# Four modulation rows moved from the projection stage into the key and value stage of a diffusion block

## The chip, the cores and the metric

One Trainium2 chip, one core. The metric is the device time of one launch in microseconds (us). The kernel is written for a scheduler: it records operations in program order, and a list scheduler sets the order of each engine's queue before the run. On the chip each engine then runs its own queue strictly in that order, and waits at an instruction until its operands are there. The engines are PE (TensorE, matmuls), DVE (VectorE), ACT (ScalarE), POOL (GpSimd) and SP, whose queue here only issues DMAs. ACT also issues DMAs, between its own instructions.

## What is computed

One layer of a hybrid block over 1024 latent tokens with 256 context tokens, model width 1024, all in float32. Cut to what matters here:

```python
sh_a, sc_a, g_a, sh_f, sc_f, g_f = modulation(c, w_mod, b_mod)      # silu(c) @ w_mod + b_mod, six rows of 1024
z = modulate(h, sh_a, sc_a) @ w_in                                  # normed tokens times one wide projection
cq, ckv, kpe, su, gm, gs = split(z)
q, k, v = mla_project(cq, ckv, kpe, ...)                            # keys and values from a compressed kv
att = block_attention(q, k, v)
s5 = s5_mixer(su_lat, su_ctx, ...)                                  # state space branch, both directions
h = layer_norm(ALPHA * h + g_a * branch_merge(att, s5, gm, gs, ...), ln1)
h = layer_norm(ALPHA * h + g_f * peer(modulate(h, sh_f, sc_f)), ln2)
```

Of the six modulation rows the first two (`sh_a`, `sc_a`) are needed before anything else. The last four (`g_a`, `sh_f`, `sc_f`, `g_f`) are first needed after attention. They come from a weight of 16 MB, `w_mod_b`, held as [2, 8, 128, 4, 512]: two halves `r` of two rows each, eight blocks `k` of 128 inputs.

## The kernel before

The tokens are ten tiles of 128: tiles 0 and 1 context, 2 to 9 latent. Four stages matter here.

**Start (to about 54 us).** `w_mod_a` (8 MB) is read and the first two rows are made (`pmr`, line 281).

**Projection stage (to about 182 us).** `project(n)` (lines 301 to 334) normalizes a token tile, transposes it on PE (`tp`, line 191), applies scale and shift into a tile `hm` on ACT (line 317) and DVE (line 319), writes `hm` to DRAM as `hm_d[n]`, and multiplies it by the state space part of `w_in` (`pc`, line 326, 32 matmuls). The result `su` goes to DRAM as `us_d`; for a context tile ACT issues eight small DMAs for that (line 332), for a latent tile one (line 334). Two buffers hold `hm`. After each tile two steps of `modulation_rows` are recorded (`MSTEP = 2`). One step reads 1 MB of `w_mod_b` into one of the four shared weight buffers `w` and runs four matmuls `pr` (line 348), each with a single column of `sil` as its stationary operand, in the four 32-column strips of PE side by side. After eight steps four DVE instructions add the bias (line 354) and the rows go to DRAM as `mod_d`. The first two state space parts (`s5_build`, matmuls `pk` line 519 and `pp` line 538) are also scheduled into this stage.

**Key and value stage (to about 470 us).** Lines 645 to 650 load two weights and then the state space inputs `U`, in eight DMAs of 384 KB, one for each of eight token phases `l`; each takes `us_d` rows of 768 bytes. `U` shares its place in memory with the projection weight `w1`, so it can't be written before the last `pc` has read `w1`. The eighth phase of `U` also needs the last `us_d` write. Then, for each tile `n`, the loop records `s5_states` (`pS`, lines 581 and 582, read `U`), `s5_build` for the next part, `s5_out` (a long row of DVE instructions, then `pY`, lines 620 to 622, then transposes `ptg`, line 637), `compress(n)` (reads `hm_d[n]` back into the `hm` buffers at line 663, matmuls `pb`, line 667, transposes `pt`, line 684), `values` (`pv`, line 695) and `keys` (`pk` from `ckvT`, line 704). DMAs of the tables `T` (line 532) wait on SP for small tables written by ACT.

**Attention of the first token tile** begins with `pa` (line 769), which reads `hm_d[2]` through a weight buffer. Three more groups of tiles, the expert retrieval and its dense part follow; they make up the rest of the time.

Of the kernel before, what the change touches and what calls it, by code (L numbers as in the profile page):

```python
# [8 lines left out]
F32 = mybir.dt.float32  # L9
# [8 lines left out]
MUL, ADD, SUB = ALU.mult, ALU.add, ALU.subtract  # L18
# [3 lines left out]
NT = 10  # L22
# [18 lines left out]
HMB = 2  # L41
# [14 lines left out]
GSTEP = 10  # L56
LSTEP = 24
RSTEP = 4
MSTEP = 2
XLOAD = 4  # L60
GSIDE = ('right', 'right', 'right', None)
CSIDE = ("right", "right", "right", None)
# [26 lines left out]
def block_kernel(ctx: ExitStack, tc: tile.TileContext, a: dict, out: bass.AP):  # L89
    nc = tc.nc  # L90
    V, S, PE, GP, SY = nc.vector, nc.scalar, nc.tensor, nc.gpsimd, nc.sync

    def pool(name, bufs=1, side=None, space=None):
        kw = {"name": name, "bufs": bufs}
        if side:
            kw["side"] = side
        if space is not None:
            kw["space"] = space
        return tc.alloc_tile_pool(**kw)
# [16 lines left out]
    eye = const.tile([128, 128], F32, tag="eye", name="eye")  # L116
# [7 lines left out]
    hm_d = tc.dram_tile([NT, 128, 8 * 128], F32, name="hm_d")  # L124
# [3 lines left out]
    mod_d = tc.dram_tile([4, D], F32, name="mod_d")  # L128
# [74 lines left out]
    def wload(src, shape):  # L203

        t = W.tile([128, 2048], F32, tag="w", bufs=WBUFS, name="w")
        n = 1
        for d in shape[1:]:
            n *= d
        names = "abcd"[:len(shape) - 1]
        dims = {names[i]: shape[i + 1] for i in range(len(names))}  # L210
        flat = " ".join(names)
        v = t[:, 0:n] if len(shape) == 2 else t[:, 0:n].rearrange(f"p ({flat}) -> p {flat}", **dims)
        last[0] = SY.dma_start(v, src)
        return v

    s5 = pool("s5")
# [6 lines left out]
    def bank(tag, name, shape=(128, 512)):  # L223

        if tag == "mm":
            turns[0] ^= turns[1]
            tag = "mm%d" % turns[0]
        return psum.tile(list(shape), F32, tag=tag, bufs={"S": 3, "acc": 2}.get(tag, 1), name=name)
# [104 lines left out]
        else:  # L333
            S.dma_start(us_d[:, :, lat, 32:160].rearrange("b p j -> p b j"), su)


    def modulation_rows():

        rows, brow = (s5.tile([128, 4, 160], F32, tag=t, bufs=2, name="rows").rearrange("p a b -> p (a b)")[:, 0:512]
                      for t in ("gr", "gi"))  # L340
        for r in range(2):
            ps = bank("acc", "pr")
            for j in range(4):
                SY.dma_start(brow[32 * j:32 * j + 1, :], a["b_row"][r, j:j + 1, :])
            for k in range(8):
                wt = wload(a["w_mod_b"][r, k], [128, 4, 512])
                for j in range(4):
                    PE.matmul(ps[32 * j:32 * j + 1, :], sil[:, k, 0:1], wt[:, j, :],
                              start=(k == 0), stop=(k == 7), tile_position=(0, 32 * j))
                yield  # L350
            for j in range(4):
                row = 2 * r + j // 2
                sl = slice(32 * j, 32 * j + 1)
                V.scalar_tensor_tensor(rows[sl, :], ps[sl, :], 1.0 if row == 2 else 0.0, brow[sl, :],
                                       op0=ADD, op1=ADD)
                SY.dma_start(mod_d[row:row + 1, (j % 2) * 512:(j % 2) * 512 + 512], rows[sl, :])

    side = modulation_rows()
    for n in range(NT):
        project(n)  # L360
        for _ in range(MSTEP):
            next(side, None)
    for _ in side:
        pass

    V.tensor_scalar(cni, cni, -1.0, None, op0=MUL)
    kf, kr, ki, pw2 = c32("kf"), c32("kr"), s5.tile([128, 32], I32, tag="ki", name="ki"), c32("pw2")
# [276 lines left out]

    w1b = [wload(a["w_in1"][:, k:k + 4, 0:384], [128, 4, 384]) for k in (0, 4)]
    wk = [wload(a["w_ukv"][:, k, :], [128, 2048]) for k in range(2)]
    U = s5.tile([128, 32, 192], F32, tag="U", name="U")
    ul = us_d.rearrange("b (g c) l j -> l c (b g) j", c=16)
    for l in range(8):
        SY.dma_start(U[16 * l:16 * l + 16], ul[l])  # L650


    SY.dma_start(qng, a["q_norm_g"])
# [5 lines left out]
    def compress(n):  # L659
        lat = n - 2  # L660
        ctxt = lat < 0
        hm = pre.tile([128, 8, 128], F32, tag="hm", bufs=HMB, name="hm")
        SY.dma_start(hm.rearrange("p a b -> p (a b)"), hm_d[n])
        pb = bank("mm", "pb")
        w = 320 if ctxt else 384
        for k in range(8):
            PE.matmul(pb[:, 0:w], hm[:, k, :], w1b[k // 4][:, k % 4, 0:w], start=(k == 0), stop=(k == 7))
        junk = pre.tile([128, 256], F32, tag="junk", name="junk")
        ss = cols.tile([128, 1], F32, tag="ss", name="ss")
        S.activation(junk, pb[:, 0:256], func=AF.Square, accum_out=ss)  # L670
        rk = rstd_of(ss, EPS, 1.0 / 256)
        nrm = pre.tile([128, 384], F32, tag="nrm", bufs=2, name="nrm")
        S.activation(nrm[:, 0:256], pb[:, 0:256], func=AF.Copy, scale=rk)
        if ctxt:
            S.copy(nrm[:, 256:320], pb[:, 256:320])
            S.copy(nrm[:, 320:384], pb[:, 256:320])
        else:
            tmp = pre.tile([128, 128], F32, tag="ktmp", name="ktmp")
            V.tensor_tensor(tmp, pb[:, 256:384], ropt[:, lat, :], op=MUL)
            V.tensor_tensor(nrm[:, 256:320], tmp[:, 0:64], tmp[:, 64:128], op=ADD)  # L680
            S.copy(nrm[:, 320:384], nrm[:, 256:320])
        pt = bank("S", "pt2", (128, 4, 128))
        for j in range(3):
            PE.transpose(pt[:, j, :], nrm[:, j * 128:(j + 1) * 128], eye)
        ko = n * 128
        for j in range(2):
            S.activation(ckvT[:, j, ko:ko + 128], pt[:, j, :], func=AF.Copy, scale=kng[:, j:j + 1])
        S.copy(kpe_h[:, ko:ko + 128], pt[:, 2, :])
        V.tensor_tensor(kpe_l[:, ko:ko + 128], pt[:, 2, :], kpe_h[:, ko:ko + 128].bitcast(F32), op=SUB)
# [11 lines left out]
    def keys(h, c0, c1):  # L701
        ps = bank("mm", "pk")
        for k in range(2):
            PE.matmul(ps[:, 0:c1 - c0], wk[k][:, h * 128:(h + 1) * 128], ckvT[:, k, c0:c1],
                      start=(k == 0), stop=(k == 1))
        kt = pre.tile([128, 512], F32, tag="kv", bufs=3, name="kt")
        S.copy(kt[:, 0:c1 - c0], ps[:, 0:c1 - c0])
        S.dma_start(k_d[h, :, c0:c1], kt[:, 0:c1 - c0])

    for n in range(NT):  # L710
        if n < 8:
            s5_states(n, parts[n])
        if n < 7:
            parts.append(s5_build(n + 1))
        if 0 < n < 9:
            s5_out(n - 1, parts[n - 1])
        compress(n)
        if n:
            values(n - 1)
        for c, n0, n1 in ((0, 4, 8), (1, 8, 10)):  # L720
            if n0 <= n < n1:
                for h in range(8 * (n - n0) // (n1 - n0), 8 * (n - n0 + 1) // (n1 - n0)):
                    keys(h, 512 * c, 512 * c + 512)
    values(NT - 1)
    for h in range(8):
        keys(h, 1024, KEYS)
    s5.release()
    pre.release()

# [857 lines left out]
```

## Time and profile before

| what | value |
|---|---|
| time, median of 3 runs | 3889.87 us (3882.73 to 3898.87) |
| time of the profiled execution | 3890.37 us |
| its span, first to last instruction | 3888.6 us |
| PE busy | 3431.8 us (88% of the span) |
| DVE busy | 3037.1 us (78%) |
| ACT busy | 1645.2 us (42%) |
| POOL busy | 1443.5 us (37%) |
| bytes moved | 1032.55 MB, mean 266 GB/s |
| mean granted TensorE clock | 0.936 of 2.4 GHz |

The shares are means over stages with different limits, so a change inside one stage is read from the rows of that stage. In a timeline row the first number is the start, the second the length, both in us; in square brackets stands how long the engine was idle just before and what ended the wait. The profile counts two records for each float32 matmul.

### The profile page before, as it was taken

How to read it: one execution, taken by the hardware profiler on the slowest of the kernel's cores; microseconds unless marked ns; L12 is line 12 of the kernel's file. 1: busy time of each engine (PE TensorE's matmuls, PEld its weight loads, DVE VectorE, ACT ScalarE, POOL GpSimd, SP SyncE). 2: the span in 40 equal slices, each digit the busy share in tenths (PEclk: the TensorE clock that was granted, in tenths of full speed). 3: DMA queues.
4: the chain of work that ended last, by engine and by line, in shares of the span. 5: the costliest groups of instructions: out<-in, count | busy, mean ns of one | idle time of the engine just before them, and what ended most of it. 6: DMA issues, size and time to landing. Idle time of an engine off the chain costs nothing.

```text
span 3888.6 us, 55690 instructions
## 1 busy us (share of the span) xinstructions
PE 3431.8 (88%) x20022; PEld 2769.1 (71%) x20022; DVE 3037.1 (78%) x7128; ACT 1645.2 (42%) x3216; POOL 1443.5 (37%) x1254
## 2 busy tenths in 40 slices
PE   5978888879779899799999798899889999999997
PEld 3745577878656688576687687677667777777885
DVE  7368656775898776889566688999999999998556
ACT  2223363441323564133498953334333344444442
POOL 5045300040554633543522102765666653442000
PEclk7988899999889999899999899899999999999998
DMA  8742375494897899978877655999999998897331
GB/s 281 223 83 71 128 268 193 159 358 167 312 347 271 313 346 339 341 280 285 309 286 310 263 179 197 353 352 336 343 350 359 345 349 297 311 336 273 115 124 71
DMA packets 348725, 1032.55 MB, mean 266 GB/s; under 512 B 46592, under 2 KB 142080, under 8 KB 322592
## 3 DMA queue, kind: packets, MB, share of 16 engines
q0 software_dynamic: 147456, 536.94, 37.8%
q1 hardware_dynamic: 164032, 462.20, 33.6%
q10 hardware_dynamic: 36960, 29.86, 2.4%
q8 instruction: 157, 2.57, 0.3%
q14 instruction: 120, 0.98, 0.1%
HBM read 961.27 MB, written 67.62 MB: 265 GB/s over the span
## 4 chain that ended last, share of the span: by engine, by line
PE 43%; issue 12%; DVE 12%; DMA 8%; ACT 5%; POOL 5%; another core or an unknown queue 0%; SPq 0%; DVEq 0%; POOLq 0%; ACTq 0%
DMA ub<-in_peer_u,ei 4%; PE turn L1234 4%; PE turn L1233 4%; POOL ub L1274 4%; PE turn L1235 4%; DVE ub L1278 4%; PE fd L1195 4%; PE fd L1196 4%; PE fd L1194 3%; PE acc L1354 2%; PE pe L1151 2%; PE pqr L1065 2%; PE po L808 2%; ACT first L1147 1%; DMA vb<-in_peer_v,eiT 1%
## 5 line engine op out<-in xcount | busy, mean ns | idle before, releaser
L1274 POOL DMA_INDIRECT ub<-in_peer_u,ei x512 | 649.2, 1268 | 1130.8 <-DVE ub L1278 350.7
L1278 DVE SCALAR_TENSOR_TENSOR ub<-ub,h 128x1024 f32<-128x1024 f32 x512 | 617.2, 1220 | 64.3 <-DMA ub<-in_peer_u,ei 55.0
L1316 POOL DMA_INDIRECT vb<-in_peer_v,ei x256 | 327.4, 1279 | 316.6 <-DVE f L1319 257.3
L1349 POOL DMA_INDIRECT vb<-in_peer_v,eiT x256 | 281.3, 1099 | 415.3 <-PE acc L1354 318.4
L1195 PE MATMUL fd<-v,kpe_l 128*128 128x512 f32 x891 | 366.8, 412 | 44.4 <-DVE kpe_l L233 44.3
L1233 PE MATMUL turn<-hh,u 128*128 128x512 f32 x1024 | 401.1, 392 | 0.2 <-ACT x L1238 0.2
L1234 PE MATMUL turn<-hh,u 128*128 128x512 f32 x1024 | 400.7, 391 | 0.1
L1235 PE MATMUL turn<-hl,u 128*128 128x512 f32 x1024 | 399.3, 390 | 0.0
L1194 PE MATMUL fd<-v,kpe_h 128*128 128x512 f32 x891 | 341.7, 404 | 35.5 <-ACT kpe_h L232 35.3
L1196 PE MATMUL fd<-v,kpe_h 128*128 128x512 f32 x891 | 359.8, 404 | 0.0
L1319 DVE SCALAR_TENSOR_TENSOR f<-vb,zz,f 128x1024 f32<-128x1024 f32 x254 | 325.3, 1281 | 4.9 <-DMA vb<-in_peer_v,ei 3.8
L233 DVE TENSOR_TENSOR u<-w,u 128x1024 fp32r<-128x1024 f32 x128 | 157.9, 1234 | 116.2 <-ACT u L232 112.7
L1195 PEld LDWEIGHTS fd<-v,kpe_l 128*128 128x128 f32 x891 | 173.5, 195 | 91.4 <-DVE kpe_l L233 52.6
L1194 PEld LDWEIGHTS fd<-v,kpe_h 128*128 128x128 f32 x891 | 170.6, 193 | 84.9 <-ACT kpe_h L232 43.3
L1233 PEld LDWEIGHTS turn<-hh,u 128*128 128x128 f32 x1024 | 192.2, 188 | 43.5 <-ACT x L1238 0.4
L1235 PEld LDWEIGHTS turn<-hl,u 128*128 128x128 f32 x1024 | 192.3, 188 | 41.9
L1234 PEld LDWEIGHTS turn<-hh,u 128*128 128x128 f32 x1024 | 192.2, 188 | 40.8 <-DVE u L233 0.5
L1238 ACT COPY x<-turn 128x512 f32<-128x512 f32 x128 | 75.0, 586 | 316.4 <-PE turn L1235 316.3
L232 ACT CAST v<-w 128x1024 fp32r<-128x1024 f32 x128 | 134.6, 1052 | 167.7 <-PE fd L1195 163.1
L1354 PE MATMUL acc<-vb,diag 128*32 128x256 f32 x2048 | 163.1, 399 | 46.7 <-DMA vb<-in_peer_v,eiT 42.2
L1148 DVE TENSOR_SCALAR second<-iota,pl 128x128 f32<-128x128 f32 x512 | 141.5, 350 | 79.4 <-PE pe L1151 65.6
L1196 PEld LDWEIGHTS fd<-v,kpe_h 128*128 128x128 f32 x891 | 173.3, 194 | 40.8
(422 smaller groups left out, 8623.7 us busy)
## 6 DMA issues: line engine op xcount, KB each, us to landing
w<-in_peer_uT SPq DMA_DIRECT2D x64, 1024.0 KB
w<-in_peer_v SPq DMA_DIRECT2D x64, 1024.0 KB
w<-in_peer_wq SPq DMA_DIRECT2D x32, 1024.0 KB
gT_d<-stage SPq DMA_DIRECT2D x16, 2048.0 KB
gt<-gT_d SPq DMA_DIRECT2D x32, 1024.0 KB
vh<-v_d SPq DMA_DIRECT2D x32, 640.0 KB
w<-k_d SPq DMA_DIRECT2D x32, 640.0 KB
w<-in_w_mod_b SPq DMA_DIRECT2D x16, 1024.0 KB
```

Source lines behind the costliest of these rows:

```text
L1194: PE.matmul(o, ah[:, ts], vh[:, cs], start=first, stop=False)
L1195: PE.matmul(o, al[:, ts], vh[:, cs], start=False, stop=False)
L1196: return PE.matmul(o, ah[:, ts], vl[:, cs], start=False, stop=final)
L1233: PE.matmul(turn, uh[:, k, :], hh[:, k, :], start=(k == 0), stop=False)
L1234: PE.matmul(turn, ul[:, k, :], hh[:, k, :], start=False, stop=False)
L1235: PE.matmul(turn, uh[:, k, :], hl[:, k, :], start=False, stop=(k == 7))
L1274: GP.indirect_dma_start(out=ub, out_offset=None, in_=a["peer_u"], in_offset=bass.IndirectOffsetOnAxis(ap=ei[:, s:s + 1], axis=0))
L1278: V.scalar_tensor_tensor(ub, ub, 1.0, h2, op0=MUL, op1=MUL, accum_out=dots[:, s:s + 1])
L1316: GP.indirect_dma_start(out=vb, out_offset=None, in_=a["peer_v"], in_offset=bass.IndirectOffsetOnAxis(ap=ei[:, s:s + 1], axis=0))
L1319: V.scalar_tensor_tensor(f, vb, z[:, s:s + 1], f, op0=MUL, op1=ADD)
L1349: GP.indirect_dma_start(out=vb, out_offset=None, in_=a["peer_v"], in_offset=bass.IndirectOffsetOnAxis(ap=eiT[:, t:t + 1], axis=0))
L1354: PE.matmul(acc[d // 2][o:o + 32, 256 * (d % 2):256 * (d % 2) + 256], dg[:, q, jj, :], vb[:, d * 256:(d + 1) * 256], start=False, stop=Fal ...
```

## The change

The rows move out of the projection loop into the loop over tiles of the key and value stage, four steps for each tile (`MSTEP = 4`). They no longer use the shared weight buffers but a pool `M` with one buffer of 512 KB: a step reads half a block (two of the four strips) into it and runs two matmuls, and the next load must wait until they have read it. The bias is no longer added by DVE: it is loaded into the same buffer and added by PE with a 1x1 weight (`eye[0:1, 0:1]`). The sums stand in a bank with the tag `S` instead of `acc`. The normed tiles of `compress` are read two tiles ahead (`load_hm`), the first two ahead of `U`; `U` is read in four parts of eight groups, eight DMAs of 96 KB each.

```diff
-MSTEP = 2
+MSTEP = 4
...
-    side = modulation_rows()
     for n in range(NT):
         project(n)
-        for _ in range(MSTEP):
-            next(side, None)
-    for _ in side:
-        pass
...
+    hms = []
+
+    def load_hm(n):
+        hms.append(pre.tile([128, 8, 128], F32, tag="hm", bufs=HMB, name="hm"))
+        SY.dma_start(hms[n].rearrange("p a b -> p (a b)"), hm_d[n])
+
+    load_hm(0)
+    load_hm(1)
     U = s5.tile([128, 32, 192], F32, tag="U", name="U")
-    ul = us_d.rearrange("b (g c) l j -> l c (b g) j", c=16)
-    for l in range(8):
-        SY.dma_start(U[16 * l:16 * l + 16], ul[l])
+    for b in range(4):
+        ul = us_d[b].rearrange("(g c) l j -> l c g j", c=16)
+        for l in range(8):
+            SY.dma_start(U[16 * l:16 * l + 16, 8 * b:8 * b + 8], ul[l])
...
-        hm = pre.tile([128, 8, 128], F32, tag="hm", bufs=HMB, name="hm")
-        SY.dma_start(hm.rearrange("p a b -> p (a b)"), hm_d[n])
+        hm = hms[n]
...
             PE.matmul(pb[:, 0:w], hm[:, k, :], w1b[k // 4][:, k % 4, 0:w], start=(k == 0), stop=(k == 7))
+        if n + 2 < NT:
+            load_hm(n + 2)
...
+    M = pool("M")
+
+    def modulation_rows():
+
+        def piece(name):
+            return M.tile([128, 2, 512], F32, tag="w", name=name)
+
+        for r in range(2):
+            ps = bank("S", "pr")
+            for k in range(8):
+                for h in range(2):
+                    wt = piece("wm")
+                    SY.dma_start(wt, a["w_mod_b"][r, k, :, 2 * h:2 * h + 2, :])
+                    for j in range(2):
+                        o = 32 * (2 * h + j)
+                        PE.matmul(ps[o:o + 1, :], sil[:, k, 0:1], wt[:, j, :], start=(k == 0), stop=False,
+                                  tile_position=(0, o))
+                    yield
+            for h in range(2):
+                br = piece("br")
+                SY.dma_start(br[0:1], a["b_row"][r:r + 1, 2 * h:2 * h + 2, :])
+                for j in range(2):
+                    o = 32 * (2 * h + j)
+                    PE.matmul(ps[o:o + 1, :], eye[0:1, 0:1], br[0:1, j, :], start=False, stop=True,
+                              tile_position=(0, o))
...
     for n in range(NT):
+        for _ in range(MSTEP):
+            next(side, None)
         if n < 8:
             s5_states(n, parts[n])
```

How the queues move: past the first group's attention and its gates the order of every engine is as before (but for one swap of two neighbours on DVE far behind). Three places follow; line numbers are those of the kernel that is shown.

SP's queue before, at the border between the projection and the key and value stage:

```order
L663 DMA hm<-hm_d 128x1024
L650 DMA U<-us_d 16x32x192 x7
L663 DMA hm<-hm_d 128x1024
L650 DMA U<-us_d 16x32x192
L663 DMA hm<-hm_d 128x1024 x4
```

and the same place now (`wm` is half a block of `w_mod_b`; the first `wm` stands far ahead, among the loads of `w_mod_a`):

```order
L624 DMA hm<-hm_d 128x1024
L213 DMA w<-in_w_ukv 128x2048
L706 DMA wm<-in_w_mod_b 128x1024
L624 DMA hm<-hm_d 128x1024
L632 DMA U<-us_d 16x8x192 x32
L706 DMA wm<-in_w_mod_b 128x1024
L624 DMA hm<-hm_d 128x1024 x2
L706 DMA wm<-in_w_mod_b 128x1024
L624 DMA hm<-hm_d 128x1024
```

The second `hm` now stands ahead of all of `U`; the third `wm` and the third `hm` stand behind all 32 parts of it.

PE's queue now, at the end of the projection and after it (before, `pb` of tile 0 stood behind the last `pc`):

```order
L191 MATMUL tp<-eye,w 128x128 x8
L709 MATMUL pr<-wm,sil 1x512 x2
L511 MATMUL pp<-eye,Er 128x128 x4
L326 MATMUL pc<-hm,w_178 128x128 x6
L648 MATMUL pb<-w,hm 128x320 x8
L326 MATMUL pc<-hm,w_178 128x128 x26
L709 MATMUL pr<-wm,sil 1x512 x2
L667 MATMUL pt_1522<-eye,nrm 128x128 x3
L648 MATMUL pb<-w,hm 128x320 x8
L678 MATMUL pv<-w,ckvT 128x512 x2
L554 MATMUL pS<-U,Pm 64x160
```

Two groups of `pr` stand ahead of the first `pS`, the other 34 (30 of `wm`, 4 of the bias) behind it, among the work of the key and value stage. The third comes some 70 matmuls further on, ahead of `pY` and of `pb` of tile 2.

PE's queue now, late in the key and value stage:

```order
L709 MATMUL pr<-wm,sil 1x512 x2
L595 MATMUL pY<-Ri,gi 128x128
L687 MATMUL pk<-ckvT,w 128x512 x2
L709 MATMUL pr<-wm,sil 1x512 x4
L610 MATMUL ptg<-eye,z 64x128 x8
```

Here two groups stand back to back; elsewhere other work stands between two groups, mostly much more than here.

SP's queue now, at the end of the stage:

```order
L724 DMA mod_d<-rows 1x512 x4
L213 DMA w<-in_w_cq 128x2x1024
L213 DMA w<-in_w_cq 128x1024
L962 DMA xr<-in_x 128x1024
L956 DMA tab<-mod_d 128x1024
L956 DMA tab<-in_ln_g 128x1024
L956 DMA tab<-in_ln_b 128x1024
L956 DMA tab<-mod_d 128x1024 x2
L868 DMA vh<-v_d 128x1280 x2
L213 DMA w<-hm_d 128x1024
```

Before, `w<-hm_d` stood right behind the two `w_cq`, and `xr` and the tables behind the first keys. The table loads wait for the rows in `mod_d`.

## Rows read from the trace of the kernel before

**Rows 1.** The page's head: span and instructions
```profile
span 3888.6 us, 55690 instructions
```
**Rows 2.** Stages: window, length, busy of PE, PEld, DVE, ACT, POOL, clock, DMA share, GB/s
```profile
54.10:182.30 128.20, 121.61 (x945) 99.59 (x946) 58.35 (x148) 30.62 (x63) 30.44 (x38) 0.90 0.72 242
182.30:218.20 35.90, 14.63 (x40) 8.02 (x39) 2.35 (x13) 3.12 (x10) 0.00 (x0) 0.71 1.03 131
218.20:235.80 17.60, 17.60 (x131) 11.88 (x130) 12.86 (x35) 7.73 (x24) 0.00 (x0) 1.00 0.23 78
235.80:470.40 234.60, 204.91 (x1052) 131.25 (x1051) 191.46 (x295) 85.98 (x214) 130.49 (x143) 0.88 0.25 79
470.40:520.00 49.60, 40.23 (x262) 36.37 (x263) 23.85 (x72) 23.75 (x64) 0.00 (x0) 0.86 0.73 270
```
**Rows 3.** PE's timeline from 182 us: start, length, line, tiles, idle before
```profile
182.22 4.47 PE L667 MATMUL pb<-w,hm 128*128 128x320 f32 x16
190.25 0.55 PE L684 MATMUL pt<-eye,nrm 128*128 128x128 f32 x3 [3.55 <-ACT nrm L673]
191.25 3.61 PE L695 MATMUL pv<-w,ckvT 128*128 128x512 f32 x4 [0.46 <-ACT ckvT L687]
212.13 6.16 PE L667 MATMUL pb<-w,hm 128*128 128x320 f32 x16 [17.26 <-DMA hm<-hm_d]
...
219.45 5.43 PE L667 MATMUL pb<-w,hm 128*128 128x384 f32 x16
...
226.87 1.88 PE L695 MATMUL pv<-w,ckvT 128*128 128x512 f32 x4
...
470.38 5.60 PE L769 MATMUL pa<-w 128*128 128x128 f32 x48 [0.74 <-ACT zt L638]
```
**Rows 4.** SP's timeline from 174 us: DMA issues
```profile
175.99 0.34 SPq L663 DMA_DIRECT2D hm<-hm_d  x1
182.42 9.54 SPq L650 DMA_DIRECT2D U<-us_d  x7
192.06 3.23 SPq L663 DMA_DIRECT2D hm<-hm_d  x1
...
466.64 0.34 SPq L213 DMA_DIRECT2D w<-hm_d  x1
```
**Rows 5.** DMA from 182.3 to 215 us: GB/s in 40 slices; issues, KB each
```profile
GB/s 0 78 222 114 97 106 142 104 120 157 231 200 95 100 117 125 118 99 117 103 126 100 110 106 127 106 99 117 114 130 97 142 177 318 303 202 176 129 156 100
...
U<-us_d SPq DMA_DIRECT2D x8, 384.0 KB
```
**Rows 6.** PE's waits from 235.8 to 470.4 us: total us, times, longest
```profile
PE ptg L637 <- DVE z L630: 10.7, 4, 4.2
PE ptg L637 <- DVE rs_y L144: 5.3, 1, 5.3
PE ptg L637 <- DVE rs_v L141: 3.7, 1, 3.7
```
**Rows 7.** PE's groups from 46 to 182 us: busy us, mean ns, idle before
```profile
L348 PE MATMUL pr<-w,sil 128*1 128x512 f32 x128 | 21.7, 640 | 0.0
```
**Rows 8.** PE's timeline in the projection stage
```profile
64.62 1.90 PE L348 MATMUL pr<-w,sil 128*1 128x512 f32 x16
...
84.53 3.38 PE L326 MATMUL pc<-hm,w 128*128 128x128 f32 x14 [3.42 <-ACT hm L317]
...
94.70 1.04 PE L348 MATMUL pr<-w,sil 128*1 128x512 f32 x8
...
113.96 1.89 PE L348 MATMUL pr<-w,sil 128*1 128x512 f32 x8
```
**Rows 9.** ACT's timeline from 60 to 92 us
```profile
65.34 9.76 ACTq L332 DMA_DIRECT2D us_d<-su  x8
...
84.02 1.85 ACT L317 ACTIVATE hm<-tp,modc 128x128 f32<-128x128 f32 x5 [8.30 <-DMA us_d<-su]
```
**Rows 10.** A stretch of the stage by windows, columns as in rows 2
```profile
266.60:280.20 13.60, 12.51 (x54) 8.42 (x54) 10.50 (x29) 3.67 (x12) 11.97 (x20) 0.50 0.10 25
```

More of the change, by code (lines that the diff above doesn't have):

```diff
@@ L334, in project @@
             S.dma_start(us_d[:, :, lat, 32:160].rearrange("b p j -> p b j"), su)
[L337 to L356, printed above, removed]
-    side = modulation_rows()
     for n in range(NT):
         project(n)
-        for _ in range(MSTEP):
-            next(side, None)
-    for _ in side:
-        pass
     V.tensor_scalar(cni, cni, -1.0, None, op0=MUL)
@@ L708, in keys @@
         S.dma_start(k_d[h, :, c0:c1], kt[:, 0:c1 - c0])
+    M = pool("M")
[20 more added lines that the diff above has]
+                              tile_position=(0, o))
+            rows = piece("rows")
+            for j in range(4):
+                row = 2 * r + j // 2
+                sl = slice(32 * j, 32 * j + 1)
+                V.tensor_scalar(rows[sl, 0, :], ps[sl, :], 1.0 if row == 2 else 0.0, None, op0=ADD)
+                SY.dma_start(mod_d[row:row + 1, (j % 2) * 512:(j % 2) * 512 + 512], rows[sl, 0, :])
+    side = modulation_rows()
     for n in range(NT):
+        for _ in range(MSTEP):
+            next(side, None)
         if n < 8:
@@ L726, in block_kernel @@
         keys(h, 1024, KEYS)
+    for _ in side:
+        pass
+    M.release()
     s5.release()
```

## The prediction

> **What bounds the kernel now.** I read the page first, for the span: 3888.6 us [rows 1]. The profiled run took 3890.37 us, so 1.8 us lie around the span, and it stands 0.5 us above the median of 3889.87; I sum against it. The change touches the first 480 us alone: behind the first group's attention and gates the engines' orders stay, so what the first 480 us gain or lose is passed on to the end as it is. Half a percent, 19.4 us, is about what a measurement here can tell from no change.
>
> Next the windows by stage [rows 2]. In the projection stage PE is busy 121.6 of 128.2 us: it is the bound there. Then come 35.9 us in which PE works 14.6. From 218.2 to 470.4 us PE is busy 222.5 of 252.2 us, and DVE 191.5 of the last 234.6: PE bounds this stage, with DVE close behind. DMA is 0.25 busy there, so there is room for the weights; what lacks is room on PE.
>
> PE's timeline shows the hole [rows 3]: behind the last `pc`, `pb` of tile 0, 3.55 us of waiting, one pair of `pv`, and 17.26 us of waiting for `hm` of tile 1. SP's timeline tells why [rows 4]: that load is issued at 192.06, behind seven of the eight big `U` loads, and `U` moves at about 100 to 120 GB/s for most of the time [rows 5]. So the hole is a queue, not a lack of work.
>
> **The change, part by part.**
>
> *Projection stage.* The `pr` groups kept PE busy 21.7 us there [rows 7]. Five of the sixteen ran between 64 and 79 us (the first two are the row at 64.62), while ACT stood in its sixteen small issues until 84.02 [rows 9]; after them PE waited 3.42 us for ACT [rows 8]. Taken away there, some 5 us of them only lengthen that wait. Two groups of the new kind stay in this stage, 1 us each. So -21.7 + 5 + 2 = -15 us. Ends: -25, if ACT's issues get quicker without the weight loads beside them and the wait goes too; -12, if more of the groups were filler.
>
> *The hole.* `pb` of tile 0 moves ahead of the last `pc`, so the 3.55 us go. `hm` of tile 1 is issued ahead of `U`, but it isn't read as early as the words say: both `hm` buffers are the projection's until the last `pc`, so its load starts then. What a lone load of 512 KB takes is bounded by `w<-hm_d`: issued at 466.64 [rows 4], used at 470.38 after only 0.74 us of waiting, and that for ACT [rows 3], so at most 3.7 us. Then `pb` of tile 1 (about 5.4, as the row at 219.45) and `pv` (1.88): PE reaches the first `pS` 11 us after the last `pc`. The first quarter of `U` needs `hm` (512 KB), the last `us_d` write (256 KB) and eight parts of 96 KB: 1.5 MB at the 115 GB/s of [rows 5] are 13.5 us, and that ends last. With the 4.5 us of `pb` of tile 0, now inside the projection, 18 us stand in place of 35.9: -18. Ends: -23 (`hm` moves faster than `U`, as the slices over 300 GB/s show) and -12 (32 small issues slow SP).
>
> *Behind U.* The third `wm` and the third `hm` stand behind the other 24 parts of `U`: 2.4 MB at 115 GB/s are 21 us, then about 2 to 3.7 us for each. PE has 17.6 us of work from 218.2 to 235.8 [rows 2]; without `pb` of tile 2 (5.43) and with some 2 us of `pk` more, it reaches the third `pr` 14 us after the first `pS`. There it waits, and everything behind it on PE, about 25 - 14 = +11 us. Ends: +3, since the `pY` that follow also wait for DVE's chain, which is as long; +14.
>
> *The groups themselves.* 34 groups of `pr` come into the stage. A group now has two matmuls, not four, but the four ran side by side: 1.04 us for eight records [rows 8]. Two strips should take as long as four, so halving the piece doubles PE's time: 34 x 1.0 = +34 us. At the lower clock a group takes 1.89 (the row at 113.96).
>
> *Waits for one buffer.* Each load waits until the `pr` before it has read. A round is issue and landing, 3.7 us at most, at least 512 KB at the 318 GB/s of the best slice in [rows 5], 1.6. Between most groups the order puts 3 to 9 us of other PE work, counted with the durations of the rows before, which hides it. One pair stands back to back and pays it whole, a few others have about 2 us of cover; SP's own waits for the tables `T` stand between some loads too. I take +8, ends +2 and +20.
>
> *What fills gaps.* From 235.8 on PE idles 29.7 us; 19.7 of them wait for DVE ahead of `ptg` [rows 6]. DVE's work stays, PE's grows, so PE comes later to these places and part of its new work costs nothing. I take half, -15; ends 0 and -28.
>
> *The clock.* PE ran at a mean of 0.88 here, in stretches at 0.50, the lower of its two levels, and such a stretch is one with little else wrong with it: 12.5 of 13.6 us busy [rows 10]. From 218.2 to 235.8, with no gap at all, it held 1.00 [rows 2]. I take no change, 0. The Trainium skill's page "TensorE: Matmul & The Clock Gate", section "HAM oscillation — how this bites in real kernels", tells of a loop in which each step waits for its DMA and PE falls to half its clock again at every step; by that rule this change would cost the clock as well, and the sum would be near 3925. The row at 212.13 agrees so far: 6.16 us after the long wait, against 5.43 for a larger `pb` later.
>
> *The start of attention.* SP now issues `xr`, five tables and two `vh`, 4.3 MB, ahead of `w<-hm_d`, the load that `pa` waits for. They can go out as soon as the state space buffers are free, and the tail of `keys` covers them: +3. Ends 0, and 16 if all of them move at 270 GB/s [rows 2] with nothing to hide them.
>
> DVE's eight bias additions become eight of the same shape, and the bias matmuls are in the 34; nothing for these.
>
> Sum: 3890.4 - 15 - 18 + 11 + 34 + 8 - 15 + 0 + 3 = **3898 us**, 8 us above the profiled run: no change that can be told.
>
> **The rivals.**
>
> *Slower: the clock (0.22).* Its place is the stage from the first `pS` to `pa`. If the many short waits at `pr` push the mean granted clock from 0.88 to 0.78, then over some 270 us this costs 270 x 0.10 = 27 us: 3925. It decides from a clock of 0.84, where 270 x 0.04 = 11 us bring the time 0.5% over the median. For it: stretches at 0.50 appear around small gaps. Against it: after the gap of 3.42 us at 84.53 PE was back at full speed by the `pr` at 94.70 [rows 8].
>
> *Faster: the gaps take it all (0.15).* If PE is held by DVE here, the new work fills its idle time: -28 for the gaps, +3 behind `U`, +3 for the rounds, -18 in the projection, -18 for the hole, +34 of work: -24, 3866. For it: the 19.7 us of waits for DVE. Against it: DVE itself idles 43 of 234.6 us [rows 2], so much of the time neither is the bound and each waits for the other in turn.
>
> *Slower: attention starts late (0.05).* The 4.3 MB ahead of `w<-hm_d` go out last and cost 16, not 3: 3911. Against it: before, that load ended no wait of PE worth naming [rows 3].
>
> *The stage is balanced otherwise (0.06).* Terms of both signs are missed by some us each, within half a percent.
>
> **How the numbers follow.** The forecast has 0.52: 3898, its own range 3882 to 3909. With the balanced case, within 0.5% has 0.58; slower 0.22 + 0.05 = 0.27; faster 0.15. The range reaches to both outer cases, 3866 to 3927; of each outer tail about one in ten lies outside.
>
> **What would show it.** Right: `hm` ends no long wait of PE after the last `pc`; the last `pc` ends 10 to 20 us earlier, the first `pS` some 33 us earlier; a wait of about 10 us for `wm` or `hm` stands ahead of `pY` and `pb` of tile 2; `pr` is busy about 34 us or more behind it; the time from the first `pS` to `pa` grows from 252 to about 290 us. Wrong: a granted clock in this stage under 0.84 or over 0.92, waits for `wm` of more than 20 us in all, `pr` groups that take half a microsecond, or a first `pa` that moves by more than 20 us either way. Behind `pa`, a shift other than that of `pa` would make the whole sum wrong.

## The result, and the profile after

The changed kernel takes **3912.21 us** (median of 5 runs, 3911.27 to 3920.29), the kernel before 3888.11 (5 runs). The ratio is 1.0065, with a 95% interval of 1.0048 to 1.0082: about 25 us slower, 19 to 32. The forecast was 3898, no change that can be told. The time lies inside the range of 3866 to 3927, but outside the likeliest case's own range of 3882 to 3909, and on the slower side.

The profiled run of the changed kernel took 3911.27 us. Its page begins:

```profile
span 3908.5 us, 55782 instructions
...
PE 3451.6 (88%) x20038; PEld 2772.2 (71%) x20038; DVE 3026.9 (77%) x7128; ACT 1645.2 (42%) x3216; POOL 1445.7 (37%) x1254
```

The span is 19.9 us longer than that of [rows 1]. The windows by stage answer to [rows 2]: the projection to the last `pc`, the hole, the first `pS` to `pa`, and the end of that stage alone, then two of the kernel before for comparison (columns: length, busy time of PE, PEld, DVE, ACT and POOL, granted clock, DMA share, GB/s):

```profile
54.10:169.90 115.80, 105.91 (x833) 100.81 (x833) 52.72 (x143) 30.09 (x65) 31.96 (x39) 0.89 0.43 131
169.90:179.10 9.20, 7.51 (x30) 4.08 (x29) 2.36 (x13) 2.43 (x7) 0.00 (x0) 1.00 0.67 138
...
179.10:485.90 306.80, 265.13 (x1316) 150.03 (x1316) 201.93 (x325) 94.39 (x236) 124.59 (x143) 0.88 0.47 142
...
451.20:485.90 34.70, 22.22 (x65) 11.39 (x64) 1.19 (x6) 9.26 (x22) 0.00 (x0) 0.91 0.72 247
```

```profile
218.20:470.40 252.20, 222.51 (x1181) 143.12 (x1180) 204.32 (x329) 93.71 (x237) 130.49 (x143) 0.89 0.25 79
...
430.00:470.40 40.40, 33.08 (x173) 21.54 (x171) 24.40 (x45) 17.36 (x39) 1.37 (x1) 1.00 0.40 137
```

The hole of 35.9 us has become 9.2, and the projection is 12.4 us shorter. Together the first `pS` comes 39.1 us earlier than in [rows 3]. But the stage behind it takes 306.8 us where it took 252.2, so `pa` comes 15.5 us later. PE's timeline at both places:

```profile
171.20 4.47 PE L648 MATMUL pb<-w,hm 128*128 128x320 f32 x16
175.51 1.88 PE L678 MATMUL pv<-w,ckvT 128*128 128x512 f32 x4
179.07 0.35 PE L554 MATMUL pS<-U,Pm 128*64 128x160 f32 x1 [1.69 <-DMA U<-us_d]
...
478.57 1.13 PE L687 MATMUL pk<-ckvT,w 128*128 128x256 f32 x4 [3.99 <-ACT kt L690]
...
485.88 1.41 PE L791 MATMUL pa<-w 128*128 128x128 f32 x5 [3.86 <-issue]
```

PE is busy 42.6 us more in the stage than before (265.1 against 222.5), 39.4 of it in `pr` (37.3 + 4.1 in the rows below, less two groups ahead of the stage), and idle 12.0 us more (41.7 against 29.7). The groups of PE's instructions:

```profile
L709 PE MATMUL pr<-wm,sil 128*1 128x512 f32 x128 | 37.3, 664 | 12.1 <-DMA wm<-in_w_mod_b 12.0
...
L717 PE MATMUL pr<-br,eye 1*1 1x512 f32 x16 | 4.1, 586 | 0.0
```

PE's waits from the first `pS` to `pa` (total, times, longest):

```profile
PE pr L709 <- DMA wm<-in_w_mod_b: 12.0, 7, 3.6
PE pk L687 <- ACT vt L681: 4.9, 5, 2.3
PE pk L687 <- ACT kt L690: 4.7, 3, 4.0
PE pk L492 <- DVE Ei L483: 4.5, 1, 4.5
...
PE ptg L610 <- DVE z L603: 3.5, 3, 2.7
...
PE ptg L610 <- DVE rs_y L144: 0.8, 1, 0.8
```

The waits of `ptg` for DVE, 19.7 us in [rows 6], are down to 4.3: the groups did fill that idle time. Part of it came back at another place, the 4.5 us that `pk` of `s5_build` waits for `Ei` (it waited 1.2 us for `Er` before); all of PE's waits for DVE in the stage together went from 20.9 to 9.6 us. Two other waits are new: 12.0 us for the weights, and those of `pk` and `pa` at the end. The window from 451.2 us shows the second: state space work is over there (DVE has 1.19 us left to do), and PE needs another 34.7 us, mostly for keys and values, 12.5 of them idle. Before, the keys were woven into the state space work and `pa` came right behind the last `ptg`; the last 40.4 us had 7.3 us of idle time. What holds the tail now stands in the queues of SP and ACT:

```profile
457.12 0.34 SPq L962 DMA_DIRECT2D xr<-in_x  x1
...
471.29 0.81 SPq L868 DMA_DIRECT2D vh<-v_d  x2
481.20 0.32 SPq L213 DMA_DIRECT2D w<-hm_d  x1
```

```profile
466.41 0.59 ACT L681 COPY vt<-pv 128x512 f32<-128x512 f32 x1 [3.81 <-DMA k_d<-kt]
...
478.15 0.37 ACT L690 COPY kt<-pk 128x256 f32<-128x256 f32 x1 [4.81 <-DMA k_d<-kt]
```

When the state space buffers come free, SP sends off the 4.3 MB for attention, between 457 and 472 us. Beside them ACT, with three buffers, waits for the writes of earlier keys and values before it can copy the next one out of PSUM, and PE waits for ACT. Before, SP issued none of these loads there, and from 430 to 470.4 us ACT's only wait for such a write was this one:

```profile
ACT kt L707 <- DMA v_d<-vt: 0.8, 1, 0.8
```

That the loads are what makes the writes late is likely, but no run takes the loads away and keeps all else.

### The profile page after: what moved, and what is told of

Same layout as the page of the kernel before. It is cut to its first block, busy times and chain, and to the rows that moved or that the text cites. A ratio compares the mean times of both kernels' runs of the same rounds, so it can differ in the third digit from the quotient of the medians.

```text
span 3908.5 us, 55782 instructions
## 1 busy us (share of the span) xinstructions
PE 3451.6 (88%) x20038; PEld 2772.2 (71%) x20038; DVE 3026.9 (77%) x7128; ACT 1645.2 (42%) x3216; POOL 1445.7 (37%) x1254
## 4 chain that ended last, share of the span: by engine, by line
PE 43%; DVE 13%; issue 12%; DMA 8%; POOL 5%; ACT 4%; SPq 0%; another core or an unknown queue 0%; POOLq 0%; DVEq 0%; ACTq 0%
DVE ub L1300 4%; POOL ub L1296 4%; PE turn L1256 4%; PE turn L1255 4%; PE turn L1257 4%; PE fd L1217 4%; PE fd L1218 3%; PE fd L1216 3%; DMA ub<-in_peer_u,ei 3%; DMA vb<-in_peer_v,eiT 2%; PE pqr L1087 2%; PE pe L1173 2%; PE acc L1376 2%; PE po L975 2%; DMA vb<-in_peer_v,ei 2%
```

## The experiments

The edits are shown in short, with the lines that matter; words in parentheses and after a semicolon are not code. All times that follow are medians; the shift is the ratio less one, times 3890 us, with its interval. "pa" is the first `pa` of the profiled run, and its shift is against 470.38. "Order" is that of the instructions on PE, DVE, ACT and SP behind 800 us: the scheduler decides it from its own clock, so a change before 480 us can alter it. Three occur: A, that of the kernel before but for neighbours (some 130 places on DVE or fewer); B and C, which differ from A and from each other in several hundred places on DVE, and little within themselves.

| kernel | first pS | pa | pa's shift | time's shift | order |
|---|---|---|---|---|---|
| before | 218.2 | 470.4 | | | A |
| changed | 179.1 | 485.9 | +15.5 | +25 (19, 32) | A |
| e1 reading ahead alone | 188.8 | 458.6 | -11.8 | +9 (3, 16) | C |
| e2 move alone | 202.7 | 489.4 | +19.0 | +48 (40, 56) | C |
| e3 bias only | 171.4 | 455.7 | -14.6 | -4 (-9, 1) | B |
| e4 resident piece | 183.5 | 484.5 | +14.1 | +25 (17, 33) | B |
| e5 four strips | 179.7 | 478.9 | +8.5 | +9 (4, 15) | A |
| e8 before, packed | 222.3 | 477.6 | +7.2 | +14 (9, 19) | B |
| e9 reading ahead, packed | 199.2 | 468.6 | -1.8 | -4 (-9, 2) | A |
| e10 resident, two a step | 181.2 | 465.3 | -5.1 | +4 (-1, 9) | A |
| e11 four strips, keys on DVE | 179.0 | 481.4 | +11.0 | +9 (4, 15) | A |
| e12 reading ahead, five kv | 198.3 | 469.9 | -0.5 | +2 (-3, 7) | A |
| e14 tile before weights | 193.8 | 458.1 | -12.3 | +9 (2, 16) | C |

### The reading ahead alone (e1)

```diff
(the kernel before)
+    load_hm(0); load_hm(1)
+    U in four parts of eight loads; hm = hms[n]; load_hm(n + 2) behind pb
```

> The kernel before with the two hm tiles read ahead and U in four parts, the modulation left in the projection stage. Theory (PE's own work bounds the key and value stage): the hole of 35.9 us between the last pc and the first pS shrinks to 12 to 18 us, the first pS comes about 20 us earlier, the stage from there to pa keeps its 252 us within 5, and the time is 3868 to 3872. Rival (DVE and the evacuations by ACT set the end of the stage, so that an earlier start is mostly given back): the stage grows by 10 us or more and the time is 3880 or above.

Measured: 3905.21 us, +9 (3 to 16). The first `pS` comes 29.4 us earlier, `pa` only 11.8, and the end later than before. The rival's bounds hold (the stage is 17.6 us longer than before, the time above 3880), but it doesn't explain an end that is later than before. The windows of the stage and of its two parts:

```profile
188.80:458.60 269.80, 223.81 (x1187) 143.02 (x1187) 205.09 (x330) 95.27 (x240) 133.40 (x143) 0.89 0.34 102
434.60:458.60 24.00, 14.99 (x46) 8.85 (x44) 0.00 (x0) 5.57 (x13) 0.00 (x0) 0.83 0.85 303
188.80:434.60 245.80, 208.82 (x1143) 134.17 (x1144) 205.09 (x330) 89.70 (x228) 133.40 (x143) 0.90 0.29 82
```

The state space work moves forward by the whole gain (its last `ptg` ends at 434.6, 35 us earlier than the 469.6 of before), but keys and values are left as a tail of 24.0 us with 9 us of idle time, at 303 GB/s. So the 29.4 us gained at the first `pS` are lost twice: 17.6 in the stage, which ends with that tail, and some 21 behind `pa`.

### The move alone (e2)

```diff
(the changed kernel)
-    load_hm ...; U in four parts
+    U in eight loads; hm read in compress(n), as before
```

> The changed kernel with U in its old eight loads and hm read where it is used, so that only the modulation rows are moved. Theory (the move alone costs about 35 us, the reading ahead gains about 20): the first pS comes some 15 us earlier than before (about 203), the stage to pa takes about 300 us, and the time is 3925 to 3935. Rival (the loads of the weights, queued ahead of hm, fill the hole with products that then cost nothing): 3905 to 3912, as the changed kernel or better.

Measured: 3944.04 us, +48, above both ranges. The first `pS` (202.7) came as expected, the stage took 286.7 us where I had said about 300, `pa` came 3.5 us later than in the changed kernel. The loads of the weights did not fill the hole: from the last `pc` to the first `pS` it is still 33.2 us. But 29 us of the +48 arise behind `pa`, as in e1.

### Bias only (e3)

```diff
(the changed kernel)
-            for k in range(8):
-                for h in range(2):
-                    wt = piece("wm"); load; two products; yield
```

> The changed kernel without the 32 loads and products of the modulation weights: only the bias rows are left (the product of the rows with their weights is left out). Theory (the groups and what they bring lengthen the stage by 35 us or more): the first pS at 176 to 180, pa at 446 to 452, so that the stage takes about 270 us where the changed kernel took 307. Rival (DVE and the evacuation of the keys would hold the stage near 300 us without the groups too): pa at 465 or later. Its order behind 800 us is that of the kernel before with three groups of pr a tile, whose end stood 2 to 8 us later than its pa.

Measured: 3878.10 us, -4 (-9 to +1). `pa` at 455.7 lies between the theories, nearer the first.

```profile
171.40:455.70 284.30, 235.97 (x1198) 147.55 (x1198) 209.65 (x338) 95.14 (x242) 129.01 (x143) 0.86 0.33 96
171.40:431.40 260.00, 220.64 (x1155) 138.48 (x1156) 209.65 (x338) 89.55 (x230) 129.01 (x143) 0.86 0.28 78
431.40:455.70 24.30, 15.33 (x45) 9.07 (x43) 0.00 (x0) 5.59 (x13) 0.00 (x0) 0.86 0.82 297
```

This is the run that splits the result. Against e3 the changed kernel's `pa` is 30.2 us later, 7.7 of it ahead of the first `pS` and 22.5 in the stage, and its time 30 us longer (1.0065 against 0.9989): that is the price of the groups in their new place (with order A against B, whose own difference the table shows to be some us). And without any products of the weights, with the first `pS` 46.8 us earlier than before, `pa` is only 14.6 us earlier: the stage has grown from 252 to 284 us, with 24.3 us of tail at its end. Of the growth 4.8 us are the bias groups, some 9 us are more busy time for the same work, at a clock of 0.86 where before had 0.89, and 18.6 us are idle time.

### One resident piece (e4, e10)

```diff
-                    wt = piece("wm")                     (for each k and h)
+            wt = piece("wm")                             (once for each r)
```

> The changed kernel with one weight piece loaded for each pair of rows and used for all sixteen of its groups: the products stay, 30 of the 32 loads and their waits go (the other fifteen pieces of weights are left out of the result). Theory (the products on PE are the larger part of the loss, the waits for wm 12 us of it): 3898 to 3904, pr still busy about 39 us, no wait for wm. Rival (the loads and the waits for the one buffer are the loss): 3880 or below.

Measured: 3922.28 us, +25, `pa` 1.4 us before that of the changed kernel. I had expected `pr` to keep its 39 us; with the piece resident, groups follow each other at once and their four strips ran side by side:

```profile
L709 PE MATMUL pr<-wm,sil 128*1 128x512 f32 x128 | 19.4, 591 | 0.0
...
L717 PE MATMUL pr<-br,eye 1*1 1x512 f32 x16 | 5.7, 803 | 0.0
```

Besides, 14 of the 32 groups ran ahead of the first `pS`, so that inside the stage `pr` is busy 17.4 us where the changed kernel had 39.4. So this run has neither the waits for `wm` nor 22 us of the products in the stage, and is no faster: in its queues other waits took their place (9.9 us of `pt` for ACT's `nrm`, 9.6 us of `pk` for `Pm`). The same kernel at two groups a tile, e10:

> The changed kernel with one resident weight piece for each pair of rows, as in the run with the resident piece, but at two groups a step, with which the order behind 800 us is nearly that of the kernel before (fifteen of sixteen pieces of the weights are left out of the result). Theory (the products keep PE, and where wm was waited for PE now waits for something else): pa at 480 to 486 us, the time within 6 us of the changed kernel, 18 to 27 us above the kernel before. Rival (the waits for the one buffer count whole): pa at 474 or earlier and the time at most 14 us above the kernel before.

Measured: 3887.49 us, +4 (-1 to 9), `pa` at 465.3, as the rival has it. But the two kernels differ only in where the groups stand, and their `pa` differs by 19 us. The stage of e4, then that of e10:

```profile
183.50:484.50 301.00, 254.64 (x1276) 155.42 (x1275) 208.38 (x338) 95.83 (x242) 127.74 (x143) 0.84 0.32 92
```

```profile
181.20:465.30 284.10, 246.34 (x1283) 149.16 (x1282) 209.12 (x338) 95.47 (x242) 136.97 (x143) 0.88 0.33 98
```

For nearly the same matmuls PE is busy 8.3 us longer in e4, at a clock of 0.84 against 0.88, and idle 8.6 us longer. So where the same work stands in this stage counts as much as how much there is of it. The pair doesn't tell the loads from their order.

### Four strips of 256 columns (e5), and keys on DVE (e11)

```diff
-                    SY.dma_start(wt, a["w_mod_b"][r, k, :, 2 * h:2 * h + 2, :])     (two strips of 512)
+                cs = slice(256 * h, 256 * h + 256)
+                    SY.dma_start(wt, a["w_mod_b"][r, k, :, :, cs])                  (four strips of 256)
```

> The changed kernel with each 512 KB piece cut the other way: four strips of 256 columns side by side where it had two strips of 512. The same bytes, loads and buffer; half the time on PE if strips run side by side. Theory (PE's time counts): pr busy falls from 39 to about 20 us, the waits for wm grow by at most 5, and the time is 3893 to 3900. Rival (the waits for the one buffer or the loads count): within 4 us of the changed kernel's 3912, or above for the shorter runs of 1 KB in each load.

Measured: 3904.81 us, ratio 1.0024 (1.0010 to 1.0038): about 16 us faster than the changed kernel (7 to 25, if the two intervals are taken as independent), as the theory has it. Same bytes, loads and buffer; on PE:

```profile
L710 PE MATMUL pr<-wm,sil 128*1 128x256 f32 x256 | 22.4, 426 | 3.3 <-DMA wm<-in_w_mod_b 3.1
...
L717 PE MATMUL pr<-br,eye 1*1 1x256 f32 x32 | 3.3, 488 | 1.1 <-DMA br<-in_b_row 1.1
```

Strips run side by side, so the shape decides: at the full clock a group takes 0.61 us where two strips of 512 took 1.03, `pr` is down by 15.7 us, and the waits for `wm`, which were to grow, fell to 3.1. But `pa` is only 7.0 us earlier than in the changed kernel, since other waits grew (9.2 us of `pk` and 6.7 us of `pp` for ACT's `ks`); the rest of the 16 us appears behind `pa`, and the runs don't say where. For the tail I then moved the last copies off ACT:

```diff
-        S.copy(kt[:, 0:c1 - c0], ps[:, 0:c1 - c0])
+        if c0 == 1024:
+            V.tensor_copy(kt[:, 0:c1 - c0], ps[:, 0:c1 - c0])
+        else:
+            S.copy(kt[:, 0:c1 - c0], ps[:, 0:c1 - c0])
```

> The kernel with four strips of 256 columns, and the eight last keys copied out of PSUM by DVE instead of ACT; the order behind 800 us is that of the kernel before but for neighbours. Theory (behind the state space work the stage ends with keys and values for which ACT is too slow, and DVE is idle there): the idle time of PE in the last 35 us before pa falls by 6 to 9 us, and the time is 0 to 6 us above the kernel before, where the four strips alone stood 10 above. Rival (the last keys wait for PE or for their writes): no change, 8 to 12 us above the kernel before.

Measured: 3892.13 us, 1.0023 (1.0009 to 1.0038), `pa` 2.5 us later than in e5: the rival. DVE waits at the same place as ACT did, for the writes (ACT's and DVE's waits from 439 to 482 us):

```profile
ACT kt L693 <- DMA v_d<-vt: 5.9, 1, 5.9
...
DVE kt L691 <- DMA k_d<-kt: 5.4, 2, 4.7
```

### The order behind 800 us (e8, e9, e14)

e8 is the kernel before, e9 the reading ahead alone, each with `MSTEP = 3` instead of 2.

> The kernel before with one number changed: three groups of pr for each projected tile where it had two. No instruction is added or left out, and the first 470 us should differ by 5 us at most. Behind 720 us, though, the order of the instructions comes out another on PE, ACT and DVE (about 470 places on DVE), as it does in the reading ahead alone, where 12 us gained at pa had become 18 us lost at the end. Theory (the order behind 720 us is what costs there): 15 to 30 us above the kernel before, nearly all of it lost between 1100 and 2700 us. Rival (that loss belongs to the earlier stage or to the single run): within 6 us of the kernel before.

Measured: 3902.33 us, +14 (9 to 19). The theory named the wrong place: `pa` was 7.2 us late already, and about 12 of the 15 us of the profiled run stood before 520 us. Order B costs little.

> The reading ahead alone once more, with three groups of pr for each projected tile; with that number the order behind 800 us is that of the kernel before but for a few neighbours. Theory (the reading ahead is worth 10 to 12 us at pa, and with the order behind it unchanged they reach the end): pa at 457 to 461 us, the time 8 to 14 us below the kernel before. Rival (an earlier start is given back behind pa whatever the order): 5 us or more above it, as in the reading ahead alone.

Measured: 3883.86 us, -4 (-9 to 2); `pa` at 468.6, not 457 to 461. Neither theory nor rival: `pa` gained only 1.8 us, since with the groups packed the last `pc` came 10 us later than in e1, and the end agrees with such a gain and with none. That left order C, and e14 was made for it:

```diff
(e9, with four buffers for keys and values)
+            hm0 = wload(hm_d[grp[0] + 2] ...)      (ahead of the two loads of w_cq, not behind them)
```

> The reading ahead alone (three groups of pr a tile, four buffers for keys and values), with the normed tile of the first attention group loaded before the weights w_cq instead of behind them, so that it takes a buffer that comes free earlier. Theory for the start of attention (pa waits for w from hm_d, whose buffer comes free only with the last keys): the wait of 6.6 us ahead of pa falls under 2 us and pa comes at 461 to 466. The order behind 800 us is that of the first run of reading ahead alone. Theory for the rest of the program (that order costs some 20 us): the time is still 8 to 20 us above the kernel before. Rival (that order costs nothing, and the first run had lost its gain otherwise): 4 to 12 us below the kernel before.

Measured: 3899.28 us, +9 (2 to 16), with `pa` 12.3 us earlier than before. All three kernels of order C (e1, e2, e14) end 21, 29 and 21 us later than their `pa` says; the kernels of order A -2 to +10, those of order B 7 to 11. So the theory fits: that order costs some 20 us. The traces show a place where it does. Matched one by one with the kernel before (median start on DVE, ACT and SP), the instructions of e1, e2 and e14 lose 15 to 19 us between 1850 and 2150 us; those of the nine other kernels in the table lose at most 5 there, or gain (those of order B lose theirs farther on, 15 to 19 us between 2150 and 2450, behind a gain). PE's waits around it, first before (1960 to 2330 us), then e14 (1950 to 2337):

```profile
PE pe L1151 <- ACT first L1149: 13.5, 9, 2.7
...
PE pe L1151 <- ACT stage L1152: 2.5, 2, 1.6
```

```profile
PE pe L1162 <- ACT stage L1163: 14.4, 5, 6.1
PE pe L1162 <- ACT first L1160: 14.1, 9, 3.6
```

The expert retrieval's `pe` waits 12 us more for ACT to empty its bank, and so it does in e1 and e2 (14.1 and 14.7 us for `stage`). But e8, with order B, has 12.5 us of that wait too, so it does not set the two orders apart; which part of the order makes the cost stays open. The start of attention went as expected, and `pa` came earlier still than 461: the wait ahead of it is gone, and a wait of 2.03 us for the last third of the weights stands inside it.

```profile
458.12 3.73 PE L780 MATMUL pa<-w 128*128 128x128 f32 x32
463.88 3.10 PE L780 MATMUL pa<-w 128*128 128x128 f32 x16 [2.03 <-DMA w<-in_w_cq]
```

### The tail: more buffers (e12), smaller pieces (e13)

```diff
(e9)
-    tag="kv", bufs=3
+    tag="kv", bufs=5
```

> The reading ahead alone (three groups of pr a tile) with five buffers for the evacuated keys and values where it had three. Theory (the last keys end late because their writes land slowly beside the loads for attention, and with three buffers the next copy waits for a write): ACT's waits for k_d and v_d in the last 24 us before pa fall from about 10 us to under 3, pa comes 4 to 8 us earlier than there (461 to 465), and the time is 6 to 12 us below the kernel before. Rival (PE or the load w that pa reads sets that end): pa moves by 2 us at most, and the time stays within 4 us of the kernel before.

Measured: 3883.01 us, +2 (-3 to 7), which is the rival's outcome. ACT's waits in the tail of e9:

```profile
ACT kt L717 <- DMA k_d<-kt: 9.8, 5, 3.3
ACT kt L717 <- DMA v_d<-vt: 3.1, 1, 3.1
```

and in e12, with PE's row at `pa`:

```profile
ACT kt L717 <- DMA tab<-mod_d: 4.1, 1, 4.1
ACT kt L717 <- DMA vh<-v_d: 1.5, 1, 1.5
...
ACT kt L717 <- DMA k_d<-kt: 1.0, 1, 1.0
```

```profile
469.86 1.41 PE L779 MATMUL pa<-w 128*128 128x128 f32 x5 [6.60 <-DMA w<-hm_d]
```

The waits under the names of `k_d` and `v_d` fell from 12.9 us to 1.0, but 5.6 us stand under the names of two loads that a copy doesn't read. ACT's timeline tells why:

```profile
454.09 0.37 ACT L717 COPY kt<-pk 128x256 f32<-128x256 f32 x1 [1.02 <-PE pk L714]
458.20 0.33 ACTq L718 DMA_DIRECT2D k_d<-kt  x1
458.57 0.37 ACT L717 COPY kt<-pk 128x256 f32<-128x256 f32 x1 [4.11 <-DMA tab<-mod_d]
```

The copy at 454.09 is done at 454.46, but ACT issues its write only at 458.20, when by the profile a load of the tables has landed, and the next copy stands behind that issue. So with the buffers there, the issue of the writes still waited for the loads. The last key ended 1.7 us earlier, but `pa` did not: it now waits 6.6 us for its own tile, which is issued behind the tables in a buffer that only the last keys set free. The rival named that load. Several waits stood one behind the other.

```diff
(the changed kernel)
-            return M.tile([128, 2, 512], F32, tag="w", name=name)      (32 pieces of 512 KB)
+            return M.tile([128, 4, 128], F32, tag="w", name=name)      (64 of 256 KB; kv bufs=4)
```

> The changed kernel with pieces of 256 KB (four strips of 128 columns, twice as many loads, a buffer of 2 KB a partition) and the room so won used for a fourth buffer of keys and values. Theory (the writes of the last keys hold the stage's end): pr busy about 22 us as with four strips of 256 columns, ACT's waits for k_d in the tail under 4 us, pa at 468 to 474 where the four strips of 256 columns had 479. Rival (the tail is set by something else, or the smaller loads cost what they save): pa at 477 or later. The order behind 800 us is another than that of the kernel before, so the time may stand up to 30 us higher than the shift of pa gives.

Measured: 3974.05 us, ratio 1.0251. `pa` came at 467.2, a little before the expected 468, but four steps a tile place only 40 of the 64 pieces in the loop. The others followed the last keys with nothing to hide them: I had not counted that, and `pr`, with many groups there at the lower clock, is busy 31.7 us instead of 22. It shows what a lone round costs, 3.6 us from one group to the next, and the clock of PE there:

```profile
472.00:574.00 102.00, 29.32 (x308) 14.17 (x306) 9.75 (x30) 5.46 (x15) 0.00 (x0) 0.58 0.33 103
```

```profile
548.32 0.60 PE L710 MATMUL pr<-wm,sil 128*1 128x128 f32 x8 [3.02 <-DMA wm<-in_w_mod_b]
551.90 0.60 PE L710 MATMUL pr<-wm,sil 128*1 128x128 f32 x8 [2.98 <-DMA wm<-in_w_mod_b]
```

## Why the prediction was right and wrong

The range held, and several terms were near; the forecast missed by 14 us, and that it missed by so little is in part luck: its 8 us came from two halves that were both too large and mostly cancelled.

- **Up to the first `pS`**: -33 forecast, -39 measured. The last `pc` came 12.4 us earlier with `pb` of tile 0 (4.5) inside it, so -17 for the projection where -15 stood. The hole lost 22 beside that `pb`, where -18 stood and -23 was the end.
- **Behind U**: +11 forecast, about +2 measured, below its end of +3. Ahead of the third group PE waits 1.6 us, and `pb` of tile 2 doesn't wait.
- **The groups**: +34 forecast, 39.4 us busy in the stage. Two strips do take as long as four did; some groups ran at the lower clock, at 1.9 us. The four strips of e5 show that this term was the shape's, not the work's.
- **Waits for one buffer**: +8 forecast, 12.0 measured, within the ends. **Gaps filled**: -15 forecast. The waits of `ptg` for DVE fell by 15.4 us, but with the new wait for `Ei` all waits for DVE fell by 11.3.
- **Clock**: 0 forecast, and the stage's clock is 0.88 against 0.89, so the rival with the clock isn't what made it slower. The rule of the Trainium skill, "TensorE: Matmul & The Clock Gate", section "HAM oscillation — how this bites in real kernels", told of a loop whose every step waits for a DMA. No stretch of the changed kernel is one, but the end of e13 is, and there the trace agrees: a mean of 0.58 over 102 us, near the lower of the two levels (0.50), against 0.86 in the stage ahead of it.
- **The start of attention**: +3 forecast, and on the slow side this term missed by most: 12.5 us of idle time stand in the tail, 3.9 of them ahead of `pa`; before, the last 40.4 us had 7.3, of which 2.0 were waits for ACT and the rest for DVE. I had seen the 4.3 MB ahead of `w<-hm_d` and wrote that the tail of `keys` covers them. It rather looks the other way round: the tail's own writes stand beside these loads, and ACT waits for them. The place was in sight: on PE's queue the keys stand behind the last `ptg`, where before that `ptg` stood right ahead of `pa`.
- **The step that failed underneath** is "PE bounds this stage", by which 33 us of earlier start were 33 us at `pa`. Without the products (e3), 46.8 us at the first `pS` are 14.6 at `pa` and 4 at the end. From the first `pS` to the last `ptg` the kernel before took 251.4 us with the keys woven in; e1 takes 245.8 and e3 260.0 for it, though some 15 us of PE's work, keys and values, have left it for the tail. So PE's own work alone did not set its length; the keys had stood in its gaps, and behind it they take time of their own. Two halves of the sum show it: all but the groups (-17 - 18 + 3 = -32) is -14.6 at `pa` and -4 at the end, and the groups with their waits (2 + 11 + 34 + 8 - 15 = +40) are +30 at both places. The sum of the two was 8 and is 25 at the end.
- **"Passed on to the end as it is"** held for the changed kernel roughly (+15.5 at `pa`, +19.9 in that profiled run, +25 by medians), whose order behind 800 us is that of before. It is false in general: order C adds some 20 us to whatever happens before 480 us. What the 4 to 10 us between `pa` and the end of the changed kernel are stays open; in the two profiled runs the shift goes from 16 us at 500 us down to 2 around 1850 and back to 19 from 2500 on, and single runs of one kernel spread by as much.
- **The other rival, gaps take it all**, falls with the 42.6 us of additional busy time of PE.

No kernel here that computes the whole result beats the one before beyond doubt. The reading ahead with the modulation left in the projection stage (e9) is at 0.9990 (0.9976 to 1.0004): no difference that can be told. The change's loss is the move (e3 without the products is 30 us faster than the changed kernel); with the pieces cut across four strips, about 16 us of it come back. How the 30 us divide between products, waits and order is not told apart: e4 has none of the waits for `wm` and less than half of the products in the stage and is no faster, while e10, with nearly the same work, is 21 us faster.

## What to carry to other kernels

Closing a hole ahead of a stage in which several engines wait for each other isn't worth the hole's length: ask what ends that stage, and when the loads of the next one are let go. Matmuls with one row of output are priced by the strips that run side by side, so cut a piece across all strips rather than along them. And where a scheduler orders the whole program, compare the orders far behind the edit before you carry a gain to the end: a different order there was worth as much as the change itself.

## What the runs showed of the hardware

Writes that land late beside loads: in the tail of e9, where 4.3 MB of loads moved, the profile could time one of the eight key writes of 128 KB, and it took 5.6 us from issue to landing. The view of DMA issues:

```profile
k_d<-kt ACTq DMA_DIRECT2D x8, 128.0 KB, 5.6
```

Giving the copies to an idle engine (e11) changed nothing that can be told, because there the buffer and not the engine was late; and more buffers (e12) moved the wait to the issue of the next write and to `pa`'s own load.
